# A store inside a load stream, split so that it falls on the first DMA engines only: row sums of 16384 x 1024 floats

## The chip, the cores and the metric

One Trainium2 chip, one core. The metric is the device time of one execution in microseconds (us), lower is better. All executions whose times are compared here are of the fast state, with a granted clock of 1.0; the four marked runs further down are single executions of unknown state, and their times are not compared. A ratio below is the mean time of one kernel's fast runs over that of the kernel before in the same rounds, so it is not quite the ratio of the medians that are quoted beside it.

## The reference, cut to what matters

```python
x = np.random.randn(32, 512, 1024).astype(np.float32)   # 67.1 MB
out = np.sum(x, axis=-1)                                # 32 x 512 sums, 64 KB
```

Each of 16384 rows of 1024 floats is summed. The input is read once; there is next to nothing to write.

## The kernel before

Rows are dealt to 128 partitions, 128 rows each, in two blocks of 112 and 16 columns. Loads go through a pool of three buffers of 16 rows. DVE reduces; near the end ACT takes part of the rows. The result of the first block is stored while the loads of the last 16 rows still stream: this is "the store in the stream".

```python
BLOCKS = (112, 16)
...
for b, n in enumerate(BLOCKS):
    x_b, out_b, res = block(done * P, n)
    ...
    while c < whole:                       # loads of 16 rows, queue of SP
        ...
        nc.sync.dma_start(out=xt[:, i * D : k * D], in_=x_b[:, (c + i) * D : (c + k) * D])
        ...
        rows_dve(xt, res, 0, m - a, c)
        rows_act(xt, res, m - a, a, c + m - a)
    if not final:
        nc.scalar.dma_start(out=out_b, in_=res)          # the store in the stream
...
cuts = [0, 9, 13, 15]                      # the last 16 rows: loads of 9, 4 and 2 rows,
for i, k in zip(cuts, cuts[1:]):           # then one row in pieces of 544 and 480 columns
    nc.sync.dma_start(...)
for i, k in ((0, CUT), (CUT, D)):
    nc.sync.dma_start(...)
... # reductions of each part as it lands; for rows 13 and 15 pairs_dve, three of them
nc.vector.tensor_copy(out=seen, in_=part)
pairs_dve(xt, last + CUT, last + D, part, res[:, c + 15 : c + 16], pairs[1])
nc.sync.dma_start(out=out_b, in_=res)      # the last store
```

## Time and profile before

| | kernel before |
|---|---|
| time, median of 3 runs | 162.24 us (162.20 to 162.41) |
| span in the profile | 160.6 us |
| load queue's share of 16 DMA engines' time | 97.2% |
| store in the stream: issued, landed | 147.87, 155.40 us |
| last load landed, DVE done, last store landed | 157.79, 158.28, 159.77 us |

The prediction shows the lines of the page, the chain of waits and the timeline. One more stretch is needed later: the timeline of the kernel before on DVE at its end. Columns: start, duration, engine, line, operation, operands, count, and in brackets the idle time before it.

```profile
156.58 0.69 DVE L59 CUSTOM_DVE_ANT_0 pairs<-xt 128x512 f32<-128x512 f32 x1 [0.25 <-DMA xt<-in_x_dram]
157.19 0.08 DVE L59 DVE_READ_ACCUMULATOR2_ANT res<- 128x1 f32 x1
157.25 0.44 DVE L59 CUSTOM_DVE_ANT_0 pairs<-xt 128x272 f32<-128x272 f32 x1
...
157.82 0.47 DVE L59 CUSTOM_DVE_ANT_0 pairs<-xt,part 128x240 f32<-128x240 f32 x1
```

The first starts when the two-row load has landed (156.55). The third, on the 544-column piece, starts at 157.25, 0.06 us after the second has started; that piece landed at 157.22. Keep this small gap in mind: the third waits for a landing. So does the last line, on the 480-column piece: that piece landed at 157.79.

Much of what follows is not in these views but in the packet records of the same trace (start, duration, bytes and queue of each DMA packet). They don't name the engine, but an engine's packets follow each other without a hole, so they can be linked to sixteen chains, one for each engine. Where an engine has moved its share of a DMA, it writes 4 bytes to a semaphore. I call the start of this packet the hand-over; the load has landed when the last of sixteen such writes has arrived.

### The profile page before, as it was taken

The page shows a single profiled execution, that of the slowest core. Times are in us where ns is not written, and L with a number is a line of the kernel's source. Part 1 is how long each engine was busy: PE and PEld are TensorE (multiplying, and loading weights), DVE is VectorE, ACT ScalarE, POOL GpSimd, SP SyncE. Part 2 cuts the span into 40 slices and gives each one's busy share as a digit, 9 for nine tenths or more (in the row PEclk, how much of TensorE's full clock was granted, in tenths as well). Part 3 has the DMA queues.
Part 4 walks back from the last instruction along what each step waited for, and adds up shares of the span by engine and source line. Part 5 has one row for each costly group of instructions (what it writes and reads, how often), then busy time and mean ns, then how long its engine had stood idle before and what let it go on. Part 6 is the DMA issues. An engine that isn't in the chain of part 4 may idle for free.

```text
span 160.6 us, 119 instructions
## 1 busy us (share of the span) xinstructions
DVE 121.5 (76%) x16; ACT 17.2 (11%) x31; POOL 0.2 (0%) x4
## 2 busy tenths in 40 slices
DVE  0000059997799959999499994999949998697884
ACT  0000000000000000000000000000000000695892
POOL 0000000000000000000000000000000000000000
DMA  9988996996996996996996996996996996998991
GB/s 375 490 367 367 490 522 277 506 522 277 506 522 261 522 522 261 522 522 261 522 506 277 522 506 277 522 506 277 522 506 277 522 490 294 441 431 364 436 390 44
DMA packets 2160, 67.18 MB, mean 418 GB/s; under 512 B 496, under 2 KB 624, under 8 KB 880
## 3 DMA queue, kind: packets, MB, share of 16 engines
q1 hardware_dynamic: 2016, 67.12, 97.2%
q10 hardware_dynamic: 144, 0.06, 0.1%
HBM read 67.11 MB, written 0.07 MB: 418 GB/s over the span
## 4 chain that ended last, share of the span: by engine, by line
DMA 75%; DVE 23%; SPq 0%; issue 0%; DVEq 0%
DMA xt<-in_x_dram 75%; DVE res L43 21%; DVE pairs L59 1%; SPq L95 0%; DVE seen L112 0%; DVE part L59 0%; DVE res L59 0%; DVEq L120 0%
## 5 line engine op out<-in xcount | busy, mean ns | idle before, releaser
L43 DVE TENSOR_REDUCE res<-xt 128x16 f32<-128x16384 f32 (+3 forms) x9 | 119.8, 13309 | 36.5 <-DMA xt<-in_x_dram 36.5
L51 ACT ACT_TABLE_LOAD x1 | 1.3, 1283 | 138.1 <-DMA xt<-in_x_dram 138.1
L51 ACT ACTIVATE xt<-xt 128x1024 f32<-128x1024 f32 x15 | 15.6, 1044 | 2.4 <-DMA xt<-in_x_dram 2.3
L51 ACT ACTIVATION_READ_ACCUMULATOR xt<-xt 128x1 f32 x15 | 2.8, 187 | 0.0
L59 DVE CUSTOM_DVE_ANT_0 pairs<-xt 128x512 f32<-128x512 f32 (+1 forms) x2 | 1.1, 567 | 0.2 <-DMA xt<-in_x_dram 0.2
L59 DVE CUSTOM_DVE_ANT_0 pairs<-xt,part 128x240 f32<-128x240 f32 x1 | 0.5, 468 | 0.0
L112 DVE COPY seen<-part 128x1 f32<-128x1 f32 x1 | 0.2, 153 | 0.0
L59 DVE DVE_READ_ACCUMULATOR2_ANT res<- 128x1 f32 x2 | 0.2, 83 | 0.0
L157 POOL MEMSET const-uint8-127<- 128x1 uint8 x1 | 0.1, 102 | 0.0
L157 POOL MEMSET const-bfloat16-1.0<- 128x1 bf16 x1 | 0.1, 101 | 0.0
L157 POOL MEMSET const-float32-0.0<- 128x1 f32 x1 | 0.1, 99 | 0.2 <-issue 0.2
L157 POOL MEMSET const-float32-1.0<- 128x1 f32 x1 | 0.1, 99 | 0.0
L59 DVE DVE_READ_ACCUMULATOR2_ANT part<- 128x1 f32 x1 | 0.1, 83 | 0.0
## 6 DMA issues: line engine op xcount, KB each, us to landing
xt<-in_x_dram SPq DMA_DIRECT2D x1, 7680.0 KB, 21.5
xt<-in_x_dram SPq DMA_DIRECT2D x1, 4608.0 KB, 32.5
xt<-in_x_dram SPq DMA_DIRECT2D x1, 2048.0 KB, 37.1
xt<-in_x_dram SPq DMA_DIRECT2D x1, 1024.0 KB, 39.1
xt<-in_x_dram SPq DMA_DIRECT2D x1, 512.0 KB, 3.8
xt<-in_x_dram SPq DMA_DIRECT2D x1, 272.0 KB, 39.3
xt<-in_x_dram SPq DMA_DIRECT2D x1, 240.0 KB, 39.4
xt<-in_x_dram SPq DMA_DIRECT2D x6, 40.8
```

Source lines behind the costliest of these rows:

```text
L43: nc.vector.tensor_reduce(out=res[:, c : c + n], in_=xt[:, j * D : (j + n) * D].rearrange("p (j d) -> p j d", d=D), axis=X, op=ADD,)
L51: nc.scalar.activation(out=v, in_=v, func=COPY, accum_out=acc)
L59: nc.vector.tensor_tensor_reduce(out=pairs[:, 0 : h - a], in0=xt[:, a:h], in1=xt[:, h:b], scale=1.0, scalar=first, op0=ADD, op1=ADD, accum ...
L112: nc.vector.tensor_copy(out=seen, in_=part)
L157: nc = _bacc.Bacc("TRN2", target_bir_lowering=False, num_devices=1)
```

## The change

The intent is to take the store off the last DMA engines, so that they fall behind less in the load stream. 104 = 13 x 8 partitions can go on 13 engines and 24 = 12 x 2 on 12.

```diff
         if not final:
-            nc.scalar.dma_start(out=out_b, in_=res)
+
+            for i, k in ((0, 104), (104, P)):
+                nc.scalar.dma_start(out=out_b[i:k], in_=res[i:k])
         done += n
```

## The prediction

> **What bounds the kernel now.** I read the page first, then the chain of waits in order of time, then the instructions of the last 15 us, then the landings. From the page of the kernel before, the DMA rows:
>
> ```profile
> DMA  9988996996996996996996996996996996998991
> ...
> q1 hardware_dynamic: 2016, 67.12, 97.2%
> q10 hardware_dynamic: 144, 0.06, 0.1%
> ...
> DMA 75%; DVE 23%; SPq 0%; issue 0%; DVEq 0%
> ```
>
> The load queue (q1) keeps the 16 DMA engines at 97.2% of the whole span; the store under change is in q10, with 0.1%. The chain is DMA for 75%; the 23% of DVE in it are two reductions during which the next load runs anyway (its own issue waited for a buffer, but loads issued before it keep the queue full). So the kernel is a load stream, and its end is what counts. The end, from the chain of waits in order of time:
>
> ```profile
> 117.43 39.13 DMA xt<-in_x_dram
> 156.55 0.02 issue
> 156.58 0.69 DVE pairs L59
> 157.27 0.01 DVE res L59
> 157.28 0.41 DVE pairs L59
> 157.69 0.02 DVE part L59
> 157.71 0.02 issue
> 157.73 0.15 DVE seen L112
> 157.88 0.40 DVE pairs L59
> 158.28 0.01 DVEq L120
> ```
>
> The reader is to see that everything from 156.55 hangs on one landing: that of the two-row load (rows 13 and 14). After it come 1.7 us of DVE without a hole, then the last store. Whatever moves this landing moves the end by as much, until another thing takes over. The timeline shows the store and its surroundings on ACT:
>
> ```profile
> 146.59 0.19 ACT L51 ACTIVATION_READ_ACCUMULATOR xt<-xt 128x1 f32 x1
> 147.87 0.37 ACTq L89 DMA_DIRECT2D out_dram<-res  x1
> 149.07 1.06 ACT L51 ACTIVATE xt<-xt 128x1024 f32<-128x1024 f32 x1 [2.29 <-DMA xt<-in_x_dram]
> 149.07 4.42 DVE L43 TENSOR_REDUCE res<-xt 128x4 f32<-128x4096 f32 x1 [1.29 <-DMA xt<-in_x_dram]
> 154.04 2.29 DVE L43 TENSOR_REDUCE res<-xt 128x2 f32<-128x2048 f32 x1 [0.55 <-DMA xt<-in_x_dram]
> ```
>
> and the DMA view says of it:
>
> ```profile
> out_dram<-res ACTq DMA_DIRECT2D x1, 56.0 KB, 7.5
> ```
>
> It is issued at 147.87, when five loads have still to land, and lands 7.5 us later, at 155.40. So its packets are moved between those of the loads, and all of them before the two-row load lands at 156.55. That is the only way in which they touch the end: they delay it.
>
> How much, I took from the trace's packet records (start, duration, bytes). The store is 128 packets of 448 bytes, eight an engine, the first at 151.37. Consecutive packets of one engine start their duration less 4 ns apart, so a 448-byte packet of 25 ns takes 21 ns of its engine's time, and the store's semaphore write of 9 ns takes 5. One engine's share is 8 x 21 + 5 = 173 ns. Following the packets from one to the next gives sixteen chains. One engine is late through the whole stream: its last packet of the nine-row load starts at 147.33, that of the next-latest engine at 147.09, and it ends its last load packet 243 ns after the next. The semaphore increments show the same: of the two-row load, fifteen have come by 156.34 and the sixteenth at 156.55; of the last piece, fifteen by 157.61 and the sixteenth at 157.79. The lag is there from the first load on (fifteen by 3.59, the last at 3.79). The end is thus set by one engine out of sixteen, by about 0.2 us.
>
> **What the Trainium skill says.** All four places are in its page "DMA: Bandwidth & Descriptors".
> - Section "Why a DMA increments its semaphore by 16 and not by 1": a DMA issued from ACT or SP uses the largest number of engines up to 16 that divides the slowest dimension of both sides, and takes the lowest-numbered ones. By this 128 partitions go on 16 engines, eight each; 104 on 13, eight each; 24 on 12, two each. The trace of before agrees for 128: sixteen increments, and eight 448-byte packets in nearly every chain that I could follow. No run shows 104 or 24 yet.
> - Section "Queues, rings and completion order": an engine takes turns between its queues, packet by packet. The trace agrees: store packets of an engine start 0.63 us apart while load packets of 16 KB (611 ns) pass, and 0.33 us apart among packets of 8 KB (309 ns).
> - Section "Latency and other measured facts": engines 7 and 15 are usually slower than the others in traces, with a cause that the page calls a guess and ties to the software-driven queues. This trace has exactly one engine that is late, but tells no engine's number, so it can't say which.
> - Section "Rules for kernel authors": two transfers to disjoint halves of the partitions are not worth it, since both run on the same engines. Here that is just what the odd sizes get round, if the first place holds.
>
> **The change, part by part.** It removes one DMA of 128 x 112 and adds one of 104 x 112 and one of 24 x 112, both on ACT's queue. The instruction streams of the two kernels differ in nothing else of substance. Comparing their waits, the completion semaphores move on by one, so that the load of the last 480 columns now waits for an old load's landing.
> 1. Packets: the same 128 of 448 bytes. Engines 0 to 11 carry 8 + 2, engine 12 carries 8, engines 13 to 15 none. Engines 0 to 11 each pay 10 x 21 + 2 x 5 = 220 ns, 47 more than before; engine 12 pays 173 as before; engines 13 to 15 save 173 ns.
> 2. Issue: one more of 0.37 us on ACT. It starts at about 148.29 and ends at about 148.7, maybe 0.1 later for the odd sizes; ACT has nothing to do until the nine-row load lands at 149.05. Hidden, with some 0.3 us to spare.
> 3. The new wait of the 480-column load: the load that it waits for (the fifth of the six of 16 rows) landed at 118.65, and this issue was at 118.41. So it is issued at about 118.7, and its packets are due only after 156.8. Hidden by 38 us.
> 4. The path to the end, if the late engine is among 13 to 15: its two-row landing goes from 156.55 to 156.38. The fifteen others come by 156.34, or 156.39 if they carry the 47 ns. So the landing is at 156.39, a gain of 0.17 us (0.166). DVE is free for it: its reduction of 2.29 us starts with the four-row landing, whose share of the saving is about half, so it ends near 156.25. The last piece lands at 157.66 at the latest instead of 157.79, while DVE's chain comes to it at 157.71: no new wait. The whole 0.17 reaches the end.
> 5. If the late engine is among 0 to 11: its landing goes to 156.60, a loss of 0.05 us. If it is engine 12: no change of its own.
>
> **The rivals.**
> (a) The late engine is among the three that are freed: 162.24 - 0.17 = 162.07 us. For it: the change frees exactly the last three, the skill names 15 as a slow one, and the lag is older than any store[...]. Against it: the trace has no engine number. I give it 60%.
> (b) The late engine is one of the first twelve, engine 7 for instance: 162.24 + 0.05 = 162.29 us. The packets that should have been relieved are then the ones that grow. 33%.
> (c) The lag is not tied to an engine but is drawn anew in each execution, or engine 12 has it: the mean lies between, from 162.1 to 162.25. The three timed executions agree within 0.21 us, which leaves room for this. 7%.
> (d) The second issue makes ACT late: it would have to cost over 0.7 us. Then ACT's five rows after 149.07 would end later; ACT is through at 156.45, 0.1 us ahead of its last row's landing, and its last row ends at 157.73 against DVE's 158.28. So even half a microsecond there would be swallowed. Cost: none.
> (e) The sum over the engines is unchanged, so a bound shared by all of them (the memory, say) would give nothing: 162.24. Against it: the late engine runs at the same pace as the others and is simply behind, and packet durations are the same on all of them by size.
>
> **Range and chances.** 0.60 x 162.07 + 0.33 x 162.29 + 0.07 x 162.2 = 162.15; I put the prediction a little to the side of the likelier case, at 162.11 us. The two cases span 162.07 to 162.29. Executions differ by 0.2 us, and the profiled one took 162.43, so I widen by 0.2 to each side: 161.87 to 162.47 should hold it 8 times in 10. A change of 2% would be 3.2 us, eighteen times the largest term of the sum; nothing in the profile offers that in either direction: 1% for each.
>
> **What would show each step right or wrong.** The DMA view should list two stores, of 45.5 and 10.5 KB, with q10 at 144 - 16 + 13 + 12 = 153 packets. The packet chains should have twelve engines with ten 448-byte packets, one with eight and three with none: that tests the rule for the number of engines. The chain that was late by 243 ns should be one of the three with none, and be late by some 25 to 70 ns afterwards; if it has ten, case (b) holds. The nine-row landing should not move against the load before it (11.04 us), since no store packet precedes it; the two-row landing should come 18.4 us after the last 16-row load's instead of 18.55. The new issue should show on ACT before 149.05, with the next activation still put down to the load. The prediction is wrong if the time moves by over 0.3 us: then a wait that I hold to be hidden is not (the moved semaphore, or the ACT issue), or stores on 13 and 12 engines are issued or landed otherwise than the one on 16.

## The result, and the profile after

| | before | changed |
|---|---|---|
| median of 6 runs | 162.29 us (162.17 to 162.41) | 162.23 us (162.15 to 162.37) |
| ratio of fast runs, 95% interval | | 0.9998 (0.9985 to 1.0011) |

The time is inside the predicted range. The 0.17 us that the likelier case promised is not there, but an interval of 0.4 us in all can't exclude it either. So the question is what became of it.

The page of the changed kernel:

```profile
DMA  9997996996996996996996979979969969998991
...
q1 hardware_dynamic: 2016, 67.12, 97.2%
q10 hardware_dynamic: 153, 0.06, 0.1%
...
DMA 75%; DVE 22%; SPq 0%; issue 0%; DVEq 0%
```

The store's queue has 153 packets, as predicted: 128 of data, and 13 + 12 semaphore writes instead of 16. The DMA view lists the two stores, without a landing time, because their semaphores don't rise in sixteen steps any more:

```profile
out_dram<-res ACTq DMA_DIRECT2D x1, 45.5 KB
out_dram<-res ACTq DMA_DIRECT2D x1, 10.5 KB
```

The timeline on ACT:

```profile
148.11 0.98 ACTq L91 DMA_DIRECT2D out_dram<-res  x2
149.19 4.42 DVE L43 TENSOR_REDUCE res<-xt 128x4 f32<-128x4096 f32 x1 [1.16 <-DMA xt<-in_x_dram]
149.20 1.06 ACT L51 ACTIVATE xt<-xt 128x1024 f32<-128x1024 f32 x1 [2.19 <-DMA xt<-in_x_dram]
```

Two issues take 0.98 us instead of 0.37; the issue on 13 engines alone takes 0.63. That is more than I estimated, and still ends at 149.10, just before the nine-row load lands at 149.16. It is hidden, with 0.06 us to spare instead of 0.3. And the end of the chain of waits:

```profile
117.65 38.95 DMA xt<-in_x_dram
156.60 0.02 issue
156.62 0.69 DVE pairs L59
157.32 0.01 DVE res L59
157.32 0.36 DVE pairs L59
```

The two-row landing, predicted at 156.39, came at 156.60: later than before (156.55). Part of it is that the stream as a whole ran late here: the last of the 16-row loads landed at 138.25 instead of 138.00, long before any store. From there to the two-row landing it took 18.35 us against 18.55, which looks like the predicted saving, but isn't all of it: 0.13 of these 0.20 us were won in the nine-row load, where no store packet moves. One pair of profiles can't tell this apart.

The chains of packets can. This is what they hold from the nine-row load's hand-over to that of the two-row load, and to that of the last piece:

```
engines with     nine-row to two-row   nine-row to last piece     profile
8 store packets          7.491 us             8.783 us            before, all sixteen engines
10                       7.539                8.831               changed, twelve engines
8                        7.491                8.783               changed, one engine
0                        7.315                8.607               changed, three engines
```

So twelve, one and three engines, as the rule quoted in the prediction has it; 48 ns paid where 47 were predicted, and 176 ns saved where 173 were. And the latest chain of the changed kernel is one of the three without a store. Step 1 of the prediction thus holds in that profile, and of step 4 the case that it rests on (the late engine is a freed one); still the end (DVE done at 158.29, before 158.28) is where it was. The theories at this point:

- A: as predicted. The gain is real, and hidden by the noise of the start.
- B: the landing of the two-row load is delayed by the second store, whose packets and semaphore writes come right ahead of it; this eats the gain.
- C: that delay was of one run only.
- D and E came up on the way: the lag of the late engine, which I took as 0.24 us, is drawn anew in each execution, and bounds the gain.

### The profile page after: what moved, and what is told of

The parts are those of the page before. It is cut to its first block, busy times and chain, and to the rows that moved or that the text cites. A ratio compares the mean times of both kernels' runs of the same rounds, so it can differ in the third digit from the quotient of the medians.

```text
span 160.6 us, 120 instructions
## 1 busy us (share of the span) xinstructions
DVE 121.4 (76%) x16; ACT 17.2 (11%) x31; POOL 0.2 (0%) x4
## 4 chain that ended last, share of the span: by engine, by line
DMA 75%; DVE 22%; SPq 0%; issue 0%; DVEq 0%
DMA xt<-in_x_dram 75%; DVE res L43 21%; DVE pairs L59 1%; SPq L97 0%; DVE seen L114 0%; DVE part L59 0%; DVEq L122 0%; DVE res L59 0%
```

## The experiments

Twelve runs. The chains were followed in each profile as above.

### The kernel before, again (a1_before_again)

No edit.

> The kernel before, unchanged, against itself: the floor of the noise. Every theory expects 162.2 to 162.4 us and a ratio of 1.000 within 0.001. Its profile is a second look at the late DMA engine. If the lateness belongs to the run (fifteen engines close together, one behind by a varying 0.1 to 0.35 us from the first load on), one chain is again late, with a lag that need not be 0.24 us.

Measured: 162.27 us, ratio 1.0003 (0.9989 to 1.0017). The noise of one comparison of five rounds is thus about 0.14% to either side, 0.2 us: more than the whole effect in question. From here on the chains of packets carry the argument, and times only bound it. In this profile all engines again take 7.491 us from the nine-row to the two-row hand-over. At the nine-row load the late engine is 0.10 us behind the next one; in the first profile of the same kernel it was 0.24.

### The changed kernel, again (a2_after_again)

No edit.

> The changed kernel, unchanged. Theory A (what the prediction said: the late engine is freed of 173 ns, the others pay 47 ns, and the gain reaches the end): 0.10 to 0.17 us under the run of the kernel before, ratio 0.999. Theory B (the packets do shift so, but the landing of the two-row load now comes right behind the second store's writes and its semaphore writes take longer, about 0.5 us instead of 0.37, which eats the gain): ratio 1.000, and in the profile again over 0.45 us from the last data packet of the two-row load to its last increment. Theory C (the longer semaphore writes in the first profile were that run's own): they are near 0.37 us here.

Measured: 162.18 us, ratio 0.9999 (0.9986 to 1.0011). Twelve engines with ten packets, one with eight, three with none again. But the latest freed engine is only 0.046 us behind the latest of those with ten (nine-row hand-over 148.333 against 148.287), and at the end the engine with ten packets is last: 157.118, where the freed one would have come in at 157.116 with its old share. Here the split gains nothing: minus 0.002 us.

B, too, shows. The last landing of the two-row load comes 0.63 us after its last hand-over. The timeline of DVE in this run:

```profile
156.47 0.69 DVE L59 CUSTOM_DVE_ANT_0 pairs<-xt 128x512 f32<-128x512 f32 x1 [0.46 <-DMA xt<-in_x_dram]
157.09 0.08 DVE L59 DVE_READ_ACCUMULATOR2_ANT res<- 128x1 f32 x1
157.09 0.43 DVE L59 CUSTOM_DVE_ANT_0 pairs<-xt 128x272 f32<-128x272 f32 x1
...
157.64 0.46 DVE L59 CUSTOM_DVE_ANT_0 pairs<-xt,part 128x240 f32<-128x240 f32 x1
```

Compare the third line with that of the kernel before: it starts at once. The 544-column piece landed at 156.94 and is not waited for; DVE itself is the late one, because the two-row landing that started it came late. The last piece, which landed at 157.53, is not waited for either. C falls, unless two runs had the same accident.

### No store in the stream (a3_no_store)

```diff
-        if not final:
-            nc.scalar.dma_start(out=out_b, in_=res)
```

The result is wrong.

> No store in the stream at all; wrong on purpose, since 112 of every 128 results are never written. The most that any placing of the store could gain. Theory A: all sixteen engines save 173 ns, so 162.24 - 0.17 = 162.07 us, ratio 0.9989. A rival by which a shared limit such as the memory sets the end: the 57 KB are 0.09% of the bytes, 0.14 us, much the same in time, so the packets decide: under A the step between the semaphore writes of the nine-row and the two-row load falls from 7.49 to about 7.32 us on every engine. If the end doesn't move at all, neither holds.

Measured: the nine-row to two-row step is 7.315 us on all sixteen engines, exactly what a freed engine has in the changed kernel. The packets' cost is thus confirmed. The time is not: 162.40 us, ratio 1.0008 (0.9995 to 1.0021), where 0.9989 was expected; the expectation was missed. Two things were found in the trace. Four engines together were late from the start here, and the last 16-row load landed at 138.16, among the latest of all profiles. And the end of the program differs: when the last store has landed, SP still checks the remaining completion semaphores in a fixed order. One check costs 0.06 us, and which of them the last store has depends on how many DMAs there are. Here two checks come after it, in the kernel before one, in the changed kernel none. So this kernel pays 0.06 us there, and the changed one saves 0.06 us that nobody had planned. 0.17 - 0.06 = 0.11 us of gain should be left, a ratio of 0.9993, just outside the interval; that the five executions drew late starts is argued, not shown.

### The whole store on one engine (a4_one_engine)

```diff
-            for i, k in ((0, 104), (104, P)):
+            for i, k in ((0, 127), (127, P)):
```

> The store split in 127 and 1 partitions. By the rule for the number of engines, 127 go on one engine with 127 packets of 21 ns, 2.7 us in all. Theory A (one engine's surplus sets the end): about 28 of them fit in turn among that engine's remaining load packets before the two-row load's end, 0.4 us after its share of before, and the rest is moved after the loads, so its load lands 0.2 to 0.4 us later and the store itself lands last, near 160.5; time up by 0.5 to 1.2 us, ratio 1.003 to 1.007. The rival (a limit shared by all engines; the number of packets and bytes is unchanged): no change, ratio 1.000. If 127 partitions were spread over many engines, also 1.000, with several chains holding 448-byte packets.

Measured: 163.18 us, ratio 1.0062 (1.0049 to 1.0075). It is clear of noise, and inside what theory A expected; a limit shared by all engines would have left it at 1.000. The bytes and the 128 data packets are the same as before. The DMA view and the end of the chain of waits:

```profile
out_dram<-res ACTq DMA_DIRECT2D x1, 55.6 KB
out_dram<-res ACTq DMA_DIRECT2D x1, 0.4 KB
out_dram<-res SPq DMA_DIRECT2D x1, 8.0 KB, 2.3
```

```profile
118.51 39.24 DMA xt<-in_x_dram
157.75 0.03 issue
157.78 0.47 DVE pairs L59
```

The last store takes 2.3 us instead of 1.4, and the chain no longer goes through the two-row load but through the last piece of 480 columns, which lands 0.34 us after its fifteenth increment. One of sixteen engines has 128 small packets: 46 of them pass before that landing, the rest one every 21 ns after it, to 159.64, in the way of the last store. One engine's surplus does set the end. In one detail I was wrong: the two-row load is not late here, since the engine that was loaded (one of the first) was ahead by enough.

### Which engine is late (m1_marked to m4_marked)

To put an engine's number on a chain, the store was split in seven, and brought forward by a first block of 64 columns.

```diff
-BLOCKS = (112, 16)
+BLOCKS = (64, 64)
...
-            for i, k in ((0, 104), (104, P)):
+            for i, k in ((0, 15), (15, 93), (93, 104), (104, 113), (113, 120), (120, 125), (125, P)):
```

> A kernel to learn which engine is late, not how fast it is. The first block is 64 columns instead of 112, so the store in the stream comes near 80 us, and it is split in 15, 78, 11, 9, 7, 5 and 3 partitions, which by the rule for the number of engines go on the lowest 15, 13, 11, 9, 7, 5 and 3 engines (one packet each, of 78 six each). The number of 256-byte packets in a chain then tells the engine: 0 is engine 15; 1 is 13 or 14; 7 is 11 or 12; 8 is 9 or 10; 9 is 7 or 8; 10 is 5 or 6; 11 is 3 or 4; 12 is 0, 1 or 2. Theory A (one of the last three is the late one): the chain that lands last before the stores has 0 or 1. Theory D (the lateness is drawn at the start of each execution and can fall on any engine): the late chain differs between the four runs of this kernel, and the last landing of the fourth load varies by some 0.1 to 0.4 us between them. A rival to both: the late one is always engine 7 or 15[...].

> The same kernel a second time. Theory A: the late chain again has 0 or 1 of the 256-byte packets. Theory D: it has another number than in the first in at least one of the three repeats.

> The same kernel a third time; expectations as for the second.

> The same kernel a fourth time; expectations as for the second.

Measured: 165.0 to 165.3 us, and only partly of use. The stores came at 97 us instead of 80, after a reduction of 17.2 us that I had forgotten, and with six more DMAs than in the kernel before a load had to wait: the fifth of the 16-row loads was issued at 99.3 us (77.9 before), so the load queue ran dry for a moment, and most of the marking packets fell into the gap where chains can't be linked. What is left is the mark of the first piece: its packet directly follows a load's end on fifteen engines and is missing on engine 15. By that, engine 15 was the last of the sixteen in the second and the fourth run, each time by 0.03 us, and not in the first and third; in the third another engine was last by 0.215 us. The rule for the number of engines is confirmed: besides one jump, the seven stores' semaphores rose in 15, 13, 11, 9, 7, 5 and 3 steps. The lag between the fifteenth and the last increment of the first load was 0.07, 0.18, 0.14 and 0.08 us. So the lag is drawn anew in each execution, as theory D has it; that it falls always on engine 7 or 15 is not supported by the first and third run unless it was 7 there, which can't be told. Which engine among 13 to 15, if any, is late is left open.

### The store brought forward, whole and split (b2_early_whole, b3_early_split)

To take the second store's end away from the two-row landing without taking the store away:

```diff
-BLOCKS = (112, 16)
+BLOCKS = (96, 32)
```

once in the kernel before, once in the changed one.

> The first block is 96 columns instead of 112, so the store in the stream comes near 118 us, 30 us before the nine-row load lands, and is not split. The same data, the same loads by size, packets of 384 bytes. The packets' cost only moves ahead: each engine pays about 170 ns between 118 and 149 us, and from the nine-row load's semaphore write to the two-row load's it takes 7.32 us, as without a store, instead of 7.49. Theory B (a store's write right ahead of a load's semaphore write makes that landing later): the two-row load lands 0.37 to 0.48 us after its last semaphore write was handed to the engines. Time against the kernel before: the same, ratio 0.999 to 1.001.

> The same early store, split in 104 and 24 partitions. Theory E (the gain of an execution is what the sum over one engine gives, at most 176 ns and at most the late engine's lead over the first twelve less 48 ns; the lag is drawn at the start of each execution): time 0 to 0.17 us below the early whole store, by how late the freed engine happens to be; ratio 0.999 to 1.000 and not clear of noise. Theory B adds: without a store near the end, the last landing of the two-row load is 0.37 to 0.48 us behind its semaphore write here, against 0.52 and 0.62 in the two profiles of the changed kernel; if it is over 0.5 here as well, B falls.

Measured: whole 162.31 us, ratio 1.0008 (0.9996 to 1.0021); split 162.12 us, ratio 0.9993 (0.9981 to 1.0005). The split one has the lowest median of all kernels, but its interval holds 1.000. The store was issued at 135.8 us, not near 118 as I had expected (I had forgotten the 17.2 us of the reduction that it waits for). With the whole store, the last data packet passed at 148.53 and the step from the nine-row to the two-row hand-over took 7.340 us, not the 7.32 expected; the split one's last semaphore write arrived at 151.3. Both are still well ahead of the two-row load. For B this is what was wanted: two-row landing 0.47 us (whole) and 0.45 us (split) after the last hand-over, against 0.52 and 0.63 in the first two profiles of the changed kernel. B stands. In the timeline of DVE of the early split one, the wait for the 544-column piece is back:

```profile
156.30 0.69 DVE L59 CUSTOM_DVE_ANT_0 pairs<-xt 128x512 f32<-128x512 f32 x1 [0.21 <-DMA xt<-in_x_dram]
156.92 0.08 DVE L59 DVE_READ_ACCUMULATOR2_ANT res<- 128x1 f32 x1
156.99 0.44 DVE L59 CUSTOM_DVE_ANT_0 pairs<-xt 128x272 f32<-128x272 f32 x1
```

### The changed kernel, a third and a fourth time (a5_after_third, a6_after_fourth)

No edit.

> The changed kernel once more, for the lag. Theory E: with the semaphore writes of the nine-row load as they come out, an engine with no store packets ends its last load 8.61 us later, one with eight 8.78, one with ten 8.83, within 0.01; the last of the sixteen sums is the last landing. Over the two earlier profiles of this kernel the latest engine was a freed one, by 0.28 us over the latest that carries packets in the first and by 0.05 in the second; here it comes out anew, anywhere from none to 0.35. Theory A (a fixed lag of 0.24 us on the same engine): 0.2 to 0.28 again. Time: 0 to 0.17 us under the kernel before.

> The same as the third, again: theory E another lag, theory A the same one as in the first profile.

Measured: 162.28 us, ratio 1.0002 (0.9990 to 1.0014), and 162.25 us, ratio 1.0000 (0.9987 to 1.0013). With these there are four profiles of the changed kernel. "Lead" is how far the latest freed engine is behind the latest with ten packets at the nine-row hand-over; "gain" is worked out in each profile as the last of the last piece's hand-overs if all engines had paid 8.783 us, less the one measured; "landing" is from the last hand-over of the two-row load to its landing, and in brackets how much longer that is than the same for the 544-column load; "DVE late" is the start of DVE's work on that piece, less its landing and the 0.025 us that DVE takes to answer it in the kernel before.

| profile | lead, us | gain, us | landing, us | DVE late, us |
|---|---|---|---|---|
| changed, first | 0.277 | 0.176 | 0.52 (+0.07) | 0.00 |
| changed, second | 0.046 | -0.002 | 0.63 (+0.20) | 0.13 |
| changed, third | 0.259 | 0.176 | 0.51 (+0.13) | 0.07 |
| changed, fourth | 0.019 | -0.029 | 0.63 (+0.22) | 0.15 |
| before, two profiles | | | 0.37, 0.48 (+0.01, -0.01) | 0 |
| no store | | | 0.43 (-0.01) | 0 |
| early, whole and split | | | 0.47, 0.45 (0.00, -0.01) | 0 |

The table decides between the theories. E holds: the gain is 176 ns if the freed engine leads by more than 0.22 us (176 + 48 ns), and a small loss if it hardly leads at all. In all four profiles the latest engine at the nine-row hand-over was a freed one, so in these four the change freed the right ones. B holds: the two-row load's landing is stretched by 0.07 to 0.22 us in the four profiles in which the second store's semaphore writes go out within about 0.1 us ahead of it (in the second, 155.820 and 155.826 on the last engine), and in none of the five others of the table, nor in the four marked runs (at most +0.02, landing 0.44 to 0.46 us). The smallest of these stretches, +0.07, is also that of the run with the store on one engine, whose store ends after the loads; there the landing itself is at 0.45 us, within the usual range. What in the memory or the semaphores makes it late is not shown, nor whether it takes the split: a whole store whose writes come right ahead of the two-row load was not tried.

Not all of "DVE late" reaches the end, since DVE still has the last piece to wait for. In the kernel before, its last reduction starts 0.025 us after the 480-column landing, and so it does in the first profile of the changed kernel; in the second, third and fourth it starts 0.109, 0.054 and 0.143 us after it. That is 0.08, 0.03 and 0.12 us late, a mean of 0.06 us over the four profiles.

## Why the prediction was right or wrong

The range held, but that proves little: the range is 0.6 us wide, and each of the cases listed, gain or loss, lies within it. By its steps:

1. Packets: right to a few ns (176 saved, 48 paid, against 173 and 47; twelve, one and three engines).
2. Issue on ACT: right that it is hidden, wrong in size. It takes 0.98 us in two instead of some 0.8 and leaves 0.06 us.
3. The moved semaphore: right as to the load (issued at 118.91, its packets due 38 us later). But the prediction stopped there. The last store's semaphore moved too, to the end of the list that SP checks, and this saves 0.06 us at the very end.
4. "The whole 0.17 reaches the end": this is the step that failed, in two terms.
   - The lag of "about 0.2 us" was taken from one trace as if it were the kernel's. It is the execution's: the lead came out as 0.28, 0.05, 0.26 and 0.02 us. Nor is it always there "from the first load on": from the last engine's hand-over to the next one's it was 0.34 us at the first load and 0.12 at the nine-row load in the first profile of the changed kernel, 0.03 and 0.11 in the third. The mean gain at the packets over four profiles is (0.176 - 0.002 + 0.176 - 0.029) / 4 = 0.08 us.
   - "So the landing is at 156.39 ... no new wait": a landing was taken as the hand-over shifted. The hand-overs shifted as worked out, but the landing of the two-row load came later after them. DVE, which in the kernel before had some 0.05 us to spare there and waited for the 544-column piece, became the later one in three of the four profiles. Its last reduction starts 0.06 us later than it could, in the mean of the four.
   - Nor was it right that everything hangs on the two-row landing alone. In the kernel before, DVE waits for two more landings after it: for that of the 544 columns (157.22; its work starts at 157.25) and for that of the 480 (157.79; its work starts at 157.82). A chain whose pieces touch can still hide such waits. In the second profile of the changed kernel, where DVE waited for neither, these two reductions start 0.62 and 0.55 us after the one before them; in the kernel before it is 0.67 and 0.57 us. So the waits are of about 0.05 and 0.02 us.
5. The case in which one of the first twelve is late (33%) did not occur in four profiles. Rival (c), to which I gave 7%, "drawn anew in each execution", was the better description of the lag.

Summed: 0.08 gained at the packets, 0.06 lost by the late landing, 0.06 gained at the program's end. About 0.08 us or 0.05% are left, an estimate from four profiles. The four comparisons gave ratios of 0.9998, 0.9999, 1.0002 and 1.0000, which is no gain that could be seen; a gain of 0.05% lies inside each of their intervals, so the times neither confirm nor refute this sum. What comes before the last loads moves more than all of this: the last of the 16-row loads landed anywhere from 137.81 to 138.25 us in the nine profiles that kept the stream's order and have no surplus on one engine.

## What to carry to other kernels

When a stream is bound by sixteen engines that each move their own share, its end is that of the latest engine, and bytes taken from the others are worth nothing; but look at several executions before you build on which engine is late and by how much. Small packets put right ahead of a load that is waited for cost twice here: their time on the engine, and a later landing. And for an effect of 0.1% compare packets in traces, since the times of five rounds settled no better than 0.13%, and check what else an added DMA moves, such as the order of the final checks.

## What the Trainium skill lacked or had wrong

- Page "DMA: Bandwidth & Descriptors", section "Latency and other measured facts": engines 7 and 15 as the usually slower ones, by its best guess because of the software-driven queues. Here only hardware-driven queues carried the data, and in four of four profiles the latest engine was one of 13 to 15; but engine 15 was last in only two of four marked runs. In the run without a store no engine moved slower: the step from the nine-row to the two-row load takes 7.315 us on every one of them. The lag of the last engine differs between executions and can change within one (0.34 us behind the next at the first load, 0.12 at the nine-row load).
- Same page, section "Why a DMA increments its semaphore by 16 and not by 1": the rule for the number of engines held for 128, 127, 104, 78, 24, 15, 11, 9, 7, 5 and 3 partitions. For one partition of 112 floats, whose slowest dimension that isn't 1 is 112 on both sides and would by the words of the rule give 16 engines, the trace has a single packet of 448 bytes and a single step of the semaphore, so one engine. (The same passage says that software can split such a row so that it spreads; that this one was not split is a guess.)
- Same page, section "Rules for kernel authors", advises against two transfers to disjoint halves of the partitions because both run on all 16 engines. With 104 and 24 partitions, which are not halves, three engines had no packet of either.
- No page has a figure for how much later a load lands when a store's writes come just ahead of it: 0.51 to 0.63 us from hand-over to landing here, against 0.37 to 0.48 us without. (Page "DMA: Bandwidth & Descriptors", section "Queues, rings and completion order", does say that an engine's semaphore increment lands only after its earlier writes, across its queues; whether that is the cause here was not tested.)
- No page has the issue's cost for other numbers of engines: 0.37 us on ACT for 128 partitions, 0.61 to 0.63 us for 104.
- No page speaks of the final checks of the completion semaphores: 0.06 us for each that comes after the last store's own. (Page "Advanced Engine Details and Errata", section "Network/Comms", has 50 to 100 ns for reading a semaphore, and 0.06 us lies within that.)
